# Feed-forward up-projection: high and low part of x in one 512-column matmul

## The chip, the cores and the metric

The kernel runs on one NeuronCore of a Trainium2 chip. The metric is the device time in microseconds (us) from the start to the end of one execution. The core has five engines that work side by side, each through its own queue in order: TensorE (PE; PEld is its loading of weights), VectorE (DVE), ScalarE (ACT), GpSimd (POOL) and SyncE (SP), which issues the DMAs. They meet at semaphores.

## The reference

Two layers of an encoder on 256 tokens of width 1024, in float32. Each layer has a group of attention heads (dense latent attention and dilated windows), with an output projection, and then a gated feed-forward network with a convolution over three neighbouring tokens:

```python
def conv_ffn(h, w_up, conv_w, conv_b, w_down):
    u = h @ w_up                                   # (256, 1024) @ (1024, 2 * 2816)
    u = lax.conv_general_dilated(u, conv_w[:, None, :], window_strides=(1,),
            padding=((1, 1),), feature_group_count=2 * D_FF, ...) + conv_b
    g, up = jnp.split(u, 2, axis=-1)
    return (jax.nn.silu(g) * up) @ w_down          # (256, 2816) @ (2816, 1024)

x = x + conv_ffn(rmsnorm(x, ffn_norm[l]), w_up[l], conv_w[l], conv_b[l], w_down[l])
```

## The kernel before, in words

Every matrix product is made of float32 operands split into a high part, rounded to the matmul's input type, and a low part, the rest. Three matmuls, high x high, high x low and low x high, are added up in one PSUM bank. The weights come from memory in tiles of 1 MB (`raw`); ScalarE makes the high part (`wh`, line 175) and VectorE the low part (`wl`, line 188), unit by unit, with six buffers of each and up to five units ahead of TensorE.

The change lies in the feed-forward stage, which takes some 190 us of each layer. Its 2816 hidden columns are worked in 22 blocks of 128, counted by j. For a block, `up` multiplies the transposed x (`sf.hi`, `sf.lo`, the tiles `xh` and `xl`; 8 k-steps of 128 features by 256 tokens) with the weights of the gate half and of the up half: 2 halves x 8 k-steps x 3 matmuls of 256 columns. Both halves stand side by side in one PSUM bank of 512 columns (only blocks 0 and 1, which begin before all of x is ready, have a bank for each half). Then `gate(j)` evacuates: VectorE multiplies the bank by `r2b`, the scale of the RMS norm for each token, into an SBUF tile of 512 columns; ScalarE applies the middle tap and the bias of the convolution; VectorE adds the other two taps (four operations, line 284), ScalarE applies SiLU, VectorE multiplies gate and up half, and ScalarE and VectorE split the product into high and low part (`mh`, `ml`). `down(j - 3)`, the down-projection of the block three before, follows each `up` on TensorE: 12 matmuls of 512 columns into four accumulators (`acc`). The last four blocks of the down-projection come at the end of the layer.

PSUM has eight banks: four `acc`, two named S (`bank()`), one A (`tbank()`) and one O (`obank()`). Before, the blocks from 3 on alternate between the two S banks, one bank per block. The 512-column SBUF tiles of `wide()` rotate through seven buffers.

Outside the attention part the order of the instructions on each engine is set by a scheduler at build time; it may put weight splits and gate steps in another order when the code changes. Calls of `W.fill` in `gate` offer it the next weight splits.

The helpers `tt` (line 275) and `stt` (284) are VectorE's two-tensor and scalar-two-tensor operations, `act` (287) is ScalarE's, `ptt` (290) POOL's two-tensor operation; a profile shows their lines.

Of the kernel before, what the change touches and what calls it, by code (L numbers as in the profile page):

```python
# [11 lines left out]
F32R = mybir.dt.float32r  # L12
I32 = mybir.dt.int32
AF = mybir.ActivationFunctionType
ALU = mybir.AluOpType
# [4 lines left out]
P = 128  # L20
LINE = 32
D_MODEL = 1024
SEQ = 256
# [9 lines left out]
NF = D_FF // P  # L33
# [198 lines left out]
def encoder(ctx: ExitStack, tc: tile.TileContext, wpk, x, prm, cst, oh, rb, pos, out):  # L232
# [4 lines left out]
    work = ctx.enter_context(tc.tile_pool(name="work", bufs=2))  # L237
# [5 lines left out]
    def nm(s):  # L243
        uid[0] += 1
        return f"{s}_{uid[0]}"

    def wide():
        return work.tile([P, 512], F32, name=nm("t2"), tag="t2", bufs=7)

    def mid():  # L250
        return work.tile([P, 256], F32, name=nm("t1"), tag="t1", bufs=9)
# [4 lines left out]
    def small(n, dt=F32):  # L256
        return work.tile([P, max(n, LINE)], dt, name=nm("s"), tag=f"s{n}_{dt}", bufs=8 if n <= 32 else 2)[:, :n]
# [4 lines left out]
    def bank():  # L262
        return psa.tile([P, 512], F32, name=nm("S"), tag="S", bufs=2)

    def tbank():
        return psa.tile([P, 512], F32, name=nm("A"), tag="A", bufs=1)

    def obank():
        return psa.tile([P, 512], F32, name=nm("O"), tag="O", bufs=1)

    def acc():
        return psa.tile([P, 512], F32, name=nm("acc"), tag="acc", bufs=4)

    def tt(o, a, b, op):
        nc.vector.tensor_tensor(out=o, in0=a, in1=b, op=op)  # L275
# [7 lines left out]
    def stt(o, a, s, b, op0, op1):  # L283
        nc.vector.scalar_tensor_tensor(out=o, in0=a, scalar=s, in1=b, op0=op0, op1=op1)  # L284

    def act(o, a, f, **kw):
        nc.scalar.activation(o, a, f, **kw)  # L287
# [15 lines left out]
    mm = nc.tensor.matmul  # L303
# [145 lines left out]

    def new_xT():  # L450
        s = State()
        s.hi = work.tile([P, 8, SEQ], F32R, name=nm("xh"), tag="xh", bufs=1)
        s.lo = work.tile([P, 8, SEQ], F32R, name=nm("xl"), tag="xl", bufs=1)
        s.ss = small(4)
        return s

# [154 lines left out]
    def layer(l, sx, late, bias):  # L611
# [346 lines left out]
        def d_end(i, t):  # L958
# [8 lines left out]
            2: [lambda: d_end(1, 0), lambda: (d_end(1, 1), d_factor(1, kd))],  # L967
        }
        sf = new_xT()
        gf = par("ffn_norm", l)  # L970
        hd = Heads(l, False, qd, kd, vd, pairs)
# [90 lines left out]
        r2b = work.tile([P, SEQ], F32, name=nm("r2b"), tag="r2b", bufs=1)  # L1062

        def ffn_scale():
            xT_stats(sf)
            ob = obank()
            dg = mid()
            for t in range(2):
                ts(dg[:, t * P:t * P + P], ident, sf.r[:, t:t + 1], ALU.mult)
            mm(ob[:, :SEQ], ones, dg, start=True, stop=True)  # L1070
            act(r2b, ob[:, :SEQ], AF.Copy)
# [4 lines left out]
        def up(j, pu, ks=range(8)):  # L1076
            for half in range(2):
                u = u_f + FFN_AT[("gate", "up")[half], j]
                hi, lo = W.get(u)
                o = pu[half][:, :SEQ] if len(pu) == 2 else pu[0][:, half * SEQ:(half + 1) * SEQ]  # L1080
                for k in ks:
                    kp = slice(k * P, k * P + P)
                    mm(o, hi[:, kp], sf.hi[:, k, :], start=k == 0, stop=False)  # L1083
                    mm(o, hi[:, kp], sf.lo[:, k, :], start=False, stop=False)  # L1084
                    mm(o, lo[:, kp], sf.hi[:, k, :], start=False, stop=k == 7)  # L1085
                if ks[-1] == 7:
                    W.done(u)

        def gate(j, pu):
            s, y = wide(), wide()  # L1090
            if len(pu) == 2:
                for g in range(2):
                    tt(s[:, g * SEQ:(g + 1) * SEQ], pu[g][:, :SEQ], r2b, ALU.mult)
            else:
                tt(s.rearrange("p (g t) -> p g t", g=2), pu[0].rearrange("p (g t) -> p g t", g=2),
                   r2b.unsqueeze(1).to_broadcast([P, 2, SEQ]), ALU.mult)
            for g in range(2):
                b = j + NF * g
                act(y[:, g * SEQ:(g + 1) * SEQ], s[:, g * SEQ:(g + 1) * SEQ], AF.Identity,
                    scale=cw[:, 44 + b:45 + b], bias=cb[:, b:b + 1])  # L1100
            W.fill(2)
            for g in range(2):
                b = j + NF * g
                yg, sg = y[:, g * SEQ:(g + 1) * SEQ], s[:, g * SEQ:(g + 1) * SEQ]
                stt(yg[:, 1:], sg[:, :SEQ - 1], cw[:, b:b + 1], yg[:, 1:], ALU.mult, ALU.add)
                stt(yg[:, :SEQ - 1], sg[:, 1:], cw[:, 88 + b:89 + b], yg[:, :SEQ - 1], ALU.mult, ALU.add)
            sl, gt = mid(), mid()
            act(sl, y[:, :SEQ], AF.Silu)
            W.fill(2)
            tt(gt, sl, y[:, SEQ:], ALU.mult)  # L1110
            m = State()
            m.hi = work.tile([P, 1, SEQ], F32R, name=nm("mh"), tag="mh", bufs=6)
            m.lo = work.tile([P, 1, SEQ], F32R, name=nm("ml"), tag="ml", bufs=6)
            act(m.hi[:, 0, :], gt, AF.Copy)
            W.fill(2)
            tt(m.lo[:, 0, :], gt, m.hi.bitcast(F32)[:, 0, :], ALU.subtract)
            gates[j] = m
# [13 lines left out]
        def down(j):  # L1131
            for t in range(2):
                for c in range(2):
                    down_mm(j, t, c)
            W.done(u_f + FFN_AT["down", j])

        first = [[acc(), acc()], [bank(), bank()]]
        for j in range(2):
            up(j, first[j], range(4))
            W.fill()  # L1140
        xT_part(sf, gf, 0, 1, tbank())
        xT_part(sf, gf, 1, 1, obank())
        for j in range(NF):
            if j < 2:
                pu = first[j]
                up(j, pu, range(4, 8))
            else:
                pu = [tbank() if j == 2 else bank()]
                up(j, pu)
            if j == 0:  # L1150
                ffn_scale()
            gate(j, pu)
            if j == 0:
                box["a"] = [[acc(), acc()], [acc(), acc()]]
            if FFN_LAG <= j < NF + FFN_LAG - FFN_HOLD:
                down(j - FFN_LAG)
        held = list(range(NF - FFN_HOLD, NF))
        last = l == DEPTH - 1
        if not last:
            sx_next = new_xT()  # L1160
            gn = par("attn_norm", l + 1)
# [20 lines left out]
        for j, t, c in order:  # L1182
# [5 lines left out]
            if (j, t, c) in ((held[0], 1, 1), (held[1], 1, 1)):  # L1188
# [3 lines left out]
                         lambda: xT_stats(sx_next)]  # L1192

    s0 = new_xT()
    late = []
    angles = rope_angles()
    bias = [bias_tables]
    for l in range(DEPTH):
        s0, late = layer(l, s0, late, bias)
        bias = []  # L1200
# [57 lines left out]
```

## Time and profile before

| | us |
|---|---|
| median of three runs | 660.03 |
| lowest, highest | 659.01, 660.3 |
| the profiled execution | 659.02 |
| its span in the trace | 657.2 |
| TensorE busy | 636.5 |
| VectorE busy | 493.7 |
| ScalarE busy | 399.6 |
| POOL busy | 67.5 |

The span is the time between the first and the last recorded instruction of the profiled execution. An engine's busy time counts the time in which at least one of its instructions is in progress; a matmul overlaps the next one, so what TensorE needs for one is read from the distance between two starts, not from its duration. Idle time of an engine that nobody waits for costs nothing.

### The profile page before, as it was taken

What the parts mean: (1) busy time and instruction counts of PE and PEld (TensorE: products, weight loads), DVE (VectorE), ACT (ScalarE), POOL (GpSimd) and SP (SyncE); (2) the same over time, 40 slices, a digit from 0 to 9 for tenths busy, and PEclk for the clock granted to TensorE, in tenths of its full rate; (3) what the DMA queues carried; (4) which work ended last, traced back from release to release, by engine and by line L of the source; (5) the groups of instructions that cost most, each with busy time, mean ns of one, the idle gap of its engine ahead of it and who ended that gap; (6) DMA issues with size and microseconds to landing.
All of it is one profiled execution on the core that took longest, in us unless ns stands there. A gap on an engine that the chain in (4) does not pass through costs nothing.

```text
span 657.2 us, 10655 instructions
## 1 busy us (share of the span) xinstructions
PE 636.5 (97%) x4018; PEld 554.3 (84%) x4018; DVE 493.7 (75%) x1006; ACT 399.6 (61%) x721; POOL 67.5 (10%) x177
## 2 busy tenths in 40 slices
PE   8989899989999999999999989999899999999997
PEld 7867676679999999999899876667899999999996
DVE  5796676677987777778699766667699777777773
ACT  6972976756755555555478467766385555555551
POOL 3850170000000000000001105400000000000000
PEclk9999999999999999999999999999899999999999
DMA  8759431252664555554347422313247545544401
GB/s 300 269 194 173 179 128 65 65 192 79 237 207 183 192 193 192 192 177 154 112 136 272 161 78 115 128 65 129 65 168 280 181 175 175 184 189 188 161 1 64
DMA packets 17708, 105.19 MB, mean 160 GB/s; under 512 B 2103, under 2 KB 3800, under 8 KB 6649
## 3 DMA queue, kind: packets, MB, share of 16 engines
q1 hardware_dynamic: 17656, 104.51, 45.9%
q8 instruction: 31, 0.51, 0.3%
q14 instruction: 21, 0.16, 0.1%
HBM read 103.20 MB, written 1.31 MB: 159 GB/s over the span
## 4 chain that ended last, share of the span: by engine, by line
PE 83%; POOL 6%; DVE 5%; ACT 2%; issue 2%; DMA 1%; SPq 1%; DVEq 0%; ACTq 0%; POOLq 0%
PE S L1085 12%; PE S L1084 12%; PE S L1083 12%; PE acc L1129 6%; PE acc L1128 6%; PE acc L1127 6%; PE acc L492 3%; PE acc L491 3%; PE acc L490 3%; PE O L600 3%; POOL s L295 3%; PE S L551 2%; PE A L591 2%; PE acc L935 2%; PE acc L938 2%; PE acc L937 2%
## 5 line engine op out<-in xcount | busy, mean ns | idle before, releaser
L175 ACT ACTIVATE wh<-raw 128x1024 fp32r<-128x1024 f32 (+3 forms) x188 | 193.2, 1036 | 110.6 <-PE S L1084 64.8
L188 DVE TENSOR_TENSOR wl<-raw,wh 128x1024 fp32r<-128x1024 f32 (+3 forms) x188 | 223.6, 1192 | 28.7 <-ACT wh L175 28.1
L1084 PE MATMUL S<-xl,wh 128*128 128x256 f32 x640 | 181.3, 284 | 0.0
L1085 PE MATMUL S<-xh,wl 128*128 128x256 f32 x640 | 180.9, 283 | 0.0
L1083 PE MATMUL S<-xh,wh 128*128 128x256 f32 x640 | 180.3, 283 | 0.0
L1084 PEld LDWEIGHTS S<-xl,wh 128*128 128x128 f32 x640 | 122.7, 192 | 1.5
L1083 PEld LDWEIGHTS S<-xh,wh 128*128 128x128 f32 x640 | 122.4, 192 | 1.6
L1085 PEld LDWEIGHTS S<-xh,wl 128*128 128x128 f32 x640 | 122.7, 192 | 0.1
L284 DVE SCALAR_TENSOR_TENSOR t<-t,prm_s,t 128x255 f32<-128x255 f32 x176 | 74.0, 480 | 1.0 <-ACT t L287 0.9
L1129 PE MATMUL acc<-wl,mh 128*128 128x512 f32 x176 | 69.3, 394 | 0.0
L1127 PE MATMUL acc<-wh,mh 128*128 128x512 f32 x176 | 69.3, 394 | 0.0
L1128 PE MATMUL acc<-wh,ml 128*128 128x512 f32 x176 | 69.2, 393 | 0.0
L490 PE MATMUL acc<-wh,xh 128*128 128x512 f32 (+2 forms) x160 | 61.3, 383 | 0.9 <-ACT nat L287 0.9
L492 PE MATMUL acc<-wl,xh 128*128 128x512 f32 (+2 forms) x160 | 58.2, 364 | 0.4 <-DVE wl L188 0.4
L491 PE MATMUL acc<-wh,xl 128*128 128x512 f32 (+2 forms) x160 | 57.8, 361 | 0.0
L287 ACT ACTIVATE t<-A 128x512 f32<-128x512 f32 (+2 forms) x56 | 28.1, 503 | 45.3 <-PE A L528 23.3
L287 ACT ACTIVATE t<-t,prm_s 128x256 f32<-128x256 f32 x88 | 47.9, 593 | 4.7 <-DVE t L275 4.7
L287 ACT ACTIVATE mh<-t 128x256 fp32r<-128x256 f32 x44 | 18.3, 416 | 47.7 <-DVE t L275 47.7
L275 DVE TENSOR_TENSOR t<-S,r2b 128x512 f32<-128x512 f32 (+1 forms) x42 | 28.0, 666 | 24.0 <-PE S L1085 24.0
L1129 PEld LDWEIGHTS acc<-wl,mh 128*128 128x128 f32 x176 | 33.1, 188 | 7.5
L1127 PEld LDWEIGHTS acc<-wh,mh 128*128 128x128 f32 x176 | 33.4, 190 | 5.9
L1128 PEld LDWEIGHTS acc<-wh,ml 128*128 128x128 f32 x176 | 33.1, 188 | 6.1
(168 smaller groups left out, 974.2 us busy)
## 6 DMA issues: line engine op xcount, KB each, us to landing
raw<-in_wpk_dram SPq DMA_DIRECT2D x86, 1024.0 KB, 4.8
raw<-in_wpk_dram SPq DMA_DIRECT2D x3, 896.0 KB, 4.6
raw<-in_wpk_dram SPq DMA_DIRECT2D x3, 768.0 KB, 4.9
raw<-in_wpk_dram SPq DMA_DIRECT2D x2, 816.0 KB, 5.9
Bn<-scr SPq DMA_DIRECT2D x8, 192.0 KB, 11.3
raw<-in_wpk_dram SPq DMA_DIRECT2D x2, 720.0 KB, 5.6
X<-in_x_dram SPq DMA_DIRECT2D x4, 256.0 KB, 5.3
raw<-in_wpk_dram SPq DMA_DIRECT2D x2, 384.0 KB, 5.6
```

Of the source, the lines that this page charges most:

```text
L175: self.nc.scalar.activation(hi[:, :n], self.raw[t][:, o:o + n], AF.Copy, scale=1.0 if g is None else g)
L188: self.nc.vector.tensor_tensor(out=lo[:, :n], in0=raw, in1=hi, op=ALU.subtract)
L287: nc.scalar.activation(o, a, f, **kw)
L490: mm(o, lhs.hi[:, k, sl], rh, start=k == 0, stop=False)
L491: mm(o, lhs.lo[:, k, sl], rh, start=False, stop=False)
L492: mm(o, lhs.hi[:, k, sl], rl, start=False, stop=k == ktot - 1)
L1083: mm(o, hi[:, kp], sf.hi[:, k, :], start=k == 0, stop=False)
L1084: mm(o, hi[:, kp], sf.lo[:, k, :], start=False, stop=False)
L1085: mm(o, lo[:, kp], sf.hi[:, k, :], start=False, stop=k == 7)
L1127: mm(o, m.hi[:, 0, sl], hi[:, cs], start=j == 0, stop=False)
L1128: mm(o, m.lo[:, 0, sl], hi[:, cs], start=False, stop=False)
L1129: mm(o, m.hi[:, 0, sl], lo[:, cs], start=False, stop=j == NF - 1)
```

## The change

The two parts of x become one tile, `xhl`, so that a k-step's high and low part can be read by one matmul of 512 columns, high part times weight in the left half of the bank and low part in the right half. The product of high x and low weight is added to the left half by a matmul of 256 columns. So a block now takes two banks, one for each half, in which left and right have still to be added: blocks with odd j use the two S banks, those with even j A and O. In `gate`, ScalarE copies the right halves to a new tile `c`, VectorE scales the left halves as before, POOL scales `c` (VectorE for the last two blocks), and the two are added by POOL for even j below 15, by VectorE otherwise.

```diff
@@ -449,8 +449,8 @@
 
     def new_xT():
         s = State()
-        s.hi = work.tile([P, 8, SEQ], F32R, name=nm("xh"), tag="xh", bufs=1)
-        s.lo = work.tile([P, 8, SEQ], F32R, name=nm("xl"), tag="xl", bufs=1)
+        s.both = work.tile([P, 2, 8, SEQ], F32R, name=nm("xhl"), tag="xhl", bufs=1)
+        s.hi, s.lo = s.both[:, 0], s.both[:, 1]
         s.ss = small(4)
         return s
 
@@ -1077,23 +1077,23 @@
             for half in range(2):
                 u = u_f + FFN_AT[("gate", "up")[half], j]
                 hi, lo = W.get(u)
-                o = pu[half][:, :SEQ] if len(pu) == 2 else pu[0][:, half * SEQ:(half + 1) * SEQ]
+                o = pu[half]
                 for k in ks:
                     kp = slice(k * P, k * P + P)
-                    mm(o, hi[:, kp], sf.hi[:, k, :], start=k == 0, stop=False)
-                    mm(o, hi[:, kp], sf.lo[:, k, :], start=False, stop=False)
-                    mm(o, lo[:, kp], sf.hi[:, k, :], start=False, stop=k == 7)
+                    mm(o.rearrange("p (g t) -> p g t", g=2), hi[:, kp], sf.both[:, :, k, :], start=k == 0, stop=False)
+                    mm(o[:, :SEQ], lo[:, kp], sf.hi[:, k, :], start=False, stop=k == 7)
                 if ks[-1] == 7:
                     W.done(u)
 
         def gate(j, pu):
-            s, y = wide(), wide()
-            if len(pu) == 2:
-                for g in range(2):
-                    tt(s[:, g * SEQ:(g + 1) * SEQ], pu[g][:, :SEQ], r2b, ALU.mult)
-            else:
-                tt(s.rearrange("p (g t) -> p g t", g=2), pu[0].rearrange("p (g t) -> p g t", g=2),
-                   r2b.unsqueeze(1).to_broadcast([P, 2, SEQ]), ALU.mult)
+            s, y, c = wide(), wide(), wide()
+            for g in range(2):
+                act(c[:, g * SEQ:(g + 1) * SEQ], pu[g][:, SEQ:], AF.Copy)
+                tt(s[:, g * SEQ:(g + 1) * SEQ], pu[g][:, :SEQ], r2b, ALU.mult)
+            side = tt if j >= NF - 2 else ptt
+            side(c.rearrange("p (g t) -> p g t", g=2), c.rearrange("p (g t) -> p g t", g=2),
+                 r2b.unsqueeze(1).to_broadcast([P, 2, SEQ]), ALU.mult)
+            (tt if j % 2 or j >= NF - 7 else ptt)(s, s, c, ALU.add)
             for g in range(2):
                 b = j + NF * g
                 act(y[:, g * SEQ:(g + 1) * SEQ], s[:, g * SEQ:(g + 1) * SEQ], AF.Identity,
@@ -1145,7 +1145,7 @@
                 pu = first[j]
                 up(j, pu, range(4, 8))
             else:
-                pu = [tbank() if j == 2 else bank()]
+                pu = [bank(), bank()] if j % 2 else [tbank(), obank()]
                 up(j, pu)
             if j == 0:
                 ffn_scale()
```

On TensorE, the end of a down step (acc) and the first k-step of the next block in layer 0 are, before (S is the bank, xh and xl the parts of x, wh and wl those of the weight, mh and ml those of the gate's product):

```order
L1128 MATMUL acc_1941<-wh_2310,ml_2143 128x512
L1129 MATMUL acc_1941<-wl_2325,mh_2142 128x512
L1083 MATMUL S_2438<-xh_894,wh_2323 128x256
L1084 MATMUL S_2438<-xl_895,wh_2323 128x256
L1085 MATMUL S_2438<-xh_894,wl_2400 128x256
L1083 MATMUL S_2438<-xh_894,wh_2323 128x256
```

and now, with the start of the second k-step:

```order
L1128 MATMUL acc_1920<-wh_2250,ml_2101 128x512
L1129 MATMUL acc_1920<-wl_2265,mh_2100 128x512
L1083 MATMUL S_2369<-xhl_893,wh_2263 128x512
L1084 MATMUL S_2369<-xhl_893,wl_2331 128x256
L1083 MATMUL S_2369<-xhl_893,wh_2263 128x512
```

Three matmuls of a k-step have become two, and one of them is of 512 columns.

On VectorE, a block in the middle of layer 0 is, before, from its evacuation (t from S and r2b) to the next one (L188 is a weight split, L284 the convolution's taps, ml the low part of the gate's product):

```order
L275 TENSOR_TENSOR t_491_2579<-S_2530,r2b_1767 128x512
L188 TENSOR_TENSOR wl_2684<-raw_2419,wh_2678 128x1024
L284 SCALAR_TENSOR_TENSOR t_492_2580<-t_491_2579,prm_s,t_492_2580 128x255 x4
L188 TENSOR_TENSOR wl_2697<-raw_2500,wh_2682 128x1024
L275 TENSOR_TENSOR t_494_2599<-t_493_2598,t_492_2580 128x256
L275 TENSOR_TENSOR ml_2609<-t_494_2599,mh_2608 128x256
L188 TENSOR_TENSOR wl_2772<-raw_2500,wh_2695 128x1024
L275 TENSOR_TENSOR t_498_2673<-S_2624,r2b_1767 128x512
```

and now a block with even j (banks A and O; the first row is its second evacuation), with the evacuations of the next, odd one (S) and its add:

```order
L275 TENSOR_TENSOR t_504_2486<-O_2453,r2b_1765 128x256
L188 TENSOR_TENSOR wl_2601<-raw_2422,wh_2586 128x1024
L284 SCALAR_TENSOR_TENSOR t_505_2487<-t_504_2486,prm_s,t_505_2487 128x255 x4
L188 TENSOR_TENSOR wl_2667<-raw_2422,wh_2599 128x1024
L275 TENSOR_TENSOR t_508_2512<-t_507_2511,t_505_2487 128x256
L275 TENSOR_TENSOR t_513_2571<-S_2537,r2b_1765 128x256
L275 TENSOR_TENSOR ml_2522<-t_508_2512,mh_2521 128x256
L275 TENSOR_TENSOR t_513_2571<-S_2538,r2b_1765 128x256
L275 TENSOR_TENSOR t_513_2571<-t_513_2571,t_515_2573 128x512
L188 TENSOR_TENSOR wl_2673<-raw_2501,wh_2665 128x1024
L284 SCALAR_TENSOR_TENSOR t_514_2572<-t_513_2571,prm_s,t_514_2572 128x255 x4
L188 TENSOR_TENSOR wl_2684<-raw_2501,wh_2671 128x1024
```

Evacuations come in twos, the add of the odd block stands between its evacuation and the next weight split, and the low part of the even block stands between the two evacuations of the odd one.

On POOL there was nothing in this stage; the same two blocks and the one behind are now:

```order
L290 TENSOR_TENSOR t_506_2488<-t_506_2488,r2b_1765 128x512
L290 TENSOR_TENSOR t_504_2486<-t_504_2486,t_506_2488 128x512
L290 TENSOR_TENSOR t_515_2573<-t_515_2573,r2b_1765 128x512
L290 TENSOR_TENSOR t_524_2656<-t_524_2656,r2b_1765 128x512
L290 TENSOR_TENSOR t_522_2654<-t_522_2654,t_524_2656 128x512
```

Scale and add of the even block, scale of the odd one (whose add is VectorE's row above), and again.

## Rows read from the trace of the kernel before

**Rows 1.** Page: busy time by engine, and the granted TensorE clock by slice.
```profile
PE 636.5 (97%) x4018; PEld 554.3 (84%) x4018; DVE 493.7 (75%) x1006; ACT 399.6 (61%) x721; POOL 67.5 (10%) x177
PEclk9999999999999999999999999999899999999999
```

**Rows 2.** Stretches: us, their length, then busy time (instructions) of PE, PEld, DVE, ACT, POOL.
```profile
220.00:240.00 20.00, 20.00 (x139) 18.62 (x139) 16.12 (x26) 11.92 (x19) 0.00 (x0) 1.00 0.56 205
480.00:500.00 20.00, 20.00 (x147) 18.96 (x146) 20.00 (x37) 15.60 (x25) 0.00 (x0) 1.00 0.54 190
```

**Rows 3.** Timeline of PE: start, duration, engine, line, operation, count.
```profile
218.89 0.39 PE L1127 MATMUL acc<-wh,mh 128*128 128x512 f32 x1
221.44 0.39 PE L1129 MATMUL acc<-wl,mh 128*128 128x512 f32 x1
221.66 0.28 PE L1083 MATMUL S<-xh,wh 128*128 128x256 f32 x1
227.42 0.39 PE L1127 MATMUL acc<-wh,mh 128*128 128x512 f32 x1
...
636.00 0.39 PE L1129 MATMUL acc<-wl,mh 128*128 128x512 f32 x1
636.22 0.28 PE L1083 MATMUL S<-xh,wh 128*128 128x256 f32 x1
```

**Rows 4.** Groups by line: engine, tiles, shapes, count | busy us, mean ns | idle before.
```profile
L287 ACT ACTIVATE mh<-O 128x256 fp32r<-128x256 f32 x16 | 6.2, 386 | 5.5 <-PE O L600 5.2
L287 ACT ACTIVATE t<-t,prm_s 128x256 f32<-128x256 f32 x88 | 47.9, 593 | 4.7 <-DVE t L275 4.7
L275 DVE TENSOR_TENSOR xl<-t,xh 128x512 fp32r<-128x512 f32 x12 | 8.3, 688 | 0.8 <-ACT xh L287 0.8
L290 POOL TENSOR_TENSOR nat<-nat,fd 128x512 f32<-128x512 f32 x8 | 8.2, 1043 | 0.3
```

**Rows 5.** Timeline of DVE: one block in the middle of the stage.
```profile
253.20 0.69 DVE L275 TENSOR_TENSOR t<-S,r2b 128x512 f32<-128x512 f32 x1 [0.61 <-PE S L1085]
254.17 1.23 DVE L188 TENSOR_TENSOR wl<-raw,wh 128x1024 fp32r<-128x1024 f32 x1 [0.28 <-ACT wh L175]
255.31 1.66 DVE L284 SCALAR_TENSOR_TENSOR t<-t,prm_s,t 128x255 f32<-128x255 f32 x4
256.89 1.22 DVE L188 TENSOR_TENSOR wl<-raw,wh 128x1024 fp32r<-128x1024 f32 x1
258.03 0.42 DVE L275 TENSOR_TENSOR t<-t,t 128x256 f32<-128x256 f32 x1
258.93 0.42 DVE L275 TENSOR_TENSOR ml<-t,mh 128x256 fp32r<-128x256 f32 x1 [0.48 <-ACT mh L287]
259.88 1.23 DVE L188 TENSOR_TENSOR wl<-raw,wh 128x1024 fp32r<-128x1024 f32 x1 [0.53 <-ACT wh L175]
261.72 0.69 DVE L275 TENSOR_TENSOR t<-S,r2b 128x512 f32<-128x512 f32 x1 [0.61 <-PE S L1085]
```

**Rows 6.** Timelines of POOL and DVE where both work.
```profile
91.68 0.24 POOL L290 TENSOR_TENSOR s<-s,s 128x16 f32<-128x16 f32 x1
92.01 1.29 POOL L295 TENSOR_SCALAR s<-s 128x16 f32<-128x16 f32 x1
92.02 1.22 DVE L188 TENSOR_TENSOR wl<-raw,wh 128x1024 fp32r<-128x1024 f32 x1
...
34.56 0.32 POOL L290 TENSOR_TENSOR s<-krs,sing 128x64 f32<-128x64 f32 x1
34.58 0.32 DVE L284 SCALAR_TENSOR_TENSOR s<-s,s 128x2 f32<-128x2 f32 x1
38.34 0.15 DVE L284 SCALAR_TENSOR_TENSOR s<-s,s 128x2 f32<-128x2 f32 x1
```

**Rows 7.** Timeline of DVE: the last gate, from its evacuation to its low part.
```profile
642.18 0.69 DVE L275 TENSOR_TENSOR t<-S,r2b 128x512 f32<-128x512 f32 x1 [2.36 <-PE S L1085]
...
646.48 0.43 DVE L275 TENSOR_TENSOR ml<-t,mh 128x256 fp32r<-128x256 f32 x1 [0.49 <-ACT mh L287]
```

## Prediction

> **What bounds the kernel now.** I read the page's table of busy time first: TensorE is busy for 97% of the span and the granted clock is at its full level in nearly every slice [rows 1]. Then the busy time by stretches, where the share of the feed-forward stage is what matters: in a steady 20 us of it TensorE has no gap at all, VectorE has 16.1, ScalarE 11.9, and GpSimd (POOL) nothing to do; early in that stage VectorE is full as well (20.0 of 20) [rows 2]. So the stage, some 190 us in each layer, runs at TensorE's pace with VectorE as the next in line.
>
> Then the timeline of TensorE. Twelve 512-column matmuls of one down step take 218.89 to 221.66, 2.77 us or 0.231 each; the 48 of 256 columns behind them take until 227.42, 5.76 us or 0.120 each [rows 3]. A feed-forward column block (a j) is 8.53 us. The step from a 512-column matmul to a 256-column one occurs 36 times, from 221.44 to 221.66 first quoted and from 636.00 to 636.22; it is 0.22 or 0.23, 0.227 in the mean [rows 3].
>
> **The change, part by part.** *Matmuls.* Per k-step and half, three matmuls of 0.120 become one of 512 columns and one of 256. A 512 with a 512 behind it takes 0.231, with a 256 behind it 0.227, which is the pairing that the new code has; I take 0.229. A step goes from 0.360 to 0.349, and there are 2 layers x 22 blocks x 2 halves x 8 = 704: 7.7 us saved, with ends of 6.3 (0.231) and 9.2 (0.227). All of it is on the path as long as TensorE stays the bound. A block becomes 16 x 0.349 + 2.77 = 8.35 us.
>
> By the Trainium skill, page "TensorE: Matmul & The Clock Gate", section "Wait — 56ns, not 53.3ns?", a warm matmul costs its columns over 2.4 GHz plus about 2.5 ns: that is 109 ns and 216 ns, and a merge of two would save only the 2.5 ns, an estimated 1.8 us in all. The rows have 120 and 231, so its numbers don't fit this data type; by its rule the change would be lost in the noise.
>
> *Banks.* The two halves of a block now take two banks, and two pairs (S, S and A, O) alternate, so a pair has to be empty when the block after next begins: two down steps and one up, 2.77 + 5.58 + 2.77 = 11.1 us after its matmuls. Before, one S bank alternated with the other, with the same distance.
>
> *ScalarE* gets two 256-column copies out of a bank per block; the nearest row is 386 ns [rows 4]: 0.8 us, on 5.1 of 8.5 (11.9 of 20) [rows 2]. It stays under TensorE.
>
> *VectorE.* The 0.69 evacuation becomes two of 256 columns (a 256-column operation is 0.42, and 0.34 from issue to issue, since neighbours overlap by 0.09: 254.17 + 1.23 against 255.31) [rows 5]. Blocks with odd j, and all from 15 on, get an add of 512 columns in SBUF, 0.69 [rows 4], 0.60 issue to issue; blocks 20 and 21 the multiplication too.
>
> *POOL* gets a 512-column multiplication for blocks 0 to 19 and an add for the even ones up to 14; the row is 1.04 us [rows 4]. Alone that is 3.1 us per pair of blocks. But a 16-column POOL operation that takes 0.24 takes 1.29 when a weight split starts with it on VectorE, and is over 0.06 after the split [rows 6]: it waits until the split is done. The other direction is shown only small: a 2-column VectorE operation takes 0.32 beside a POOL operation of 0.32, against 0.15 elsewhere [rows 6]. If that holds for a long one, VectorE and POOL take turns.
>
> That is what the Trainium skill says, page "SBUF — State Buffer", section "Who interferes with whom": a VectorE operation with two SBUF inputs and a POOL operation that reads SBUF exclude each other for a whole instruction. The trace agrees for POOL's wait (1.29 against 0.24).
>
> So I walk a pair of blocks (even, then odd) through the order of the queues. VectorE's own issue distances: 6 weight splits x 1.14, 8 scalar-tensor operations in 2 x 1.58 (255.31 to 256.89), 2 products, 2 low parts and 4 evacuations x 0.34, one add 0.60: 13.3 us. Three POOL operations, 3.1. Together 16.4 against TensorE's pair of 16.7. On top come waits in queue order: the even block's convolution cannot start until copy, POOL product, POOL add and a ScalarE step (0.4 + 1.04 + 1.04 + 0.6) [rows 4] are through, with only two splits to fill that time. Behind the waiting convolution stand the next splits and the next block's evacuation; behind ScalarE's step, which waits for the add, stand the next high part (five units ahead, so TensorE does not feel it) and the SiLU. In the walk the pair comes to 16.3 us where a POOL operation that waits gets the next turn, and to 17.1 where VectorE's next split slips in ahead of it. I take the first. From block 15 on the POOL add is gone and a pair is 15.9.
>
> *Start of the stage.* VectorE is already full there [rows 2]. From the end of block 0's gate half TensorE needs 15.6 us to the end of block 3 (1.4 + 2.8 + 0.2 + 2 x 5.6). VectorE, from one high part (1.1) later, has in the new order 8 splits (9.1), 3 convolutions (4.7), 13 operations of 0.34 (4.4) and an add (0.6) to issue before that block's evacuation is done, 18.8, and five POOL operations (5.2) take turns with it, about four fifths of them outside its other waits: 24 us, or 8.5 behind the matmuls, inside the 11.1. Block 3 itself waits about 0.5 us for block 1's banks; against it, TensorE no longer waits for the second half of x, transposed earlier now. I cost the start at 0 (-0.6 to +1.3 a layer).
>
> *End of the layer.* The last gate took 642.18 to 646.91 before, 4.7 us [rows 7]; with a multiplication and an add on VectorE it is 6.1 behind the last matmul. TensorE has nine groups of three down matmuls (0.69 each) to fill 6.2 us, so the chain as such is just hidden, but every us that VectorE is still behind counts. It is 8.5 behind at block 3, gains 0.4 per pair up to block 14 (2.2), 0.8 per pair from 15 to 19 (2.0), and about 2 in the last two, which have short splits and no POOL: 2.2 us are left and show as a wait of TensorE at the end of each layer. With pairs of 17.1 it loses 1.9 instead of gaining 2.2, and 6.4 are left. Without the taking of turns nothing is left.
>
> **Sum.** 7.7 saved, 2 x 2.2 given back: -3.3. The profiled execution took 659.02 us (span 657.2); it becomes 655.7. The median of the runs is 660.03, 1.0 above the profiled one, so the forecast is 656.7. Its own range is 654 to 658.7 (savings of 6.3 to 9.2, a wait of 1.5 to 3 a layer).
>
> **Rivals.** *Slower: POOL and VectorE take turns the bad way.* Pairs at 17.1 leave 6.4 us at the end of each layer, and blocks early in the stage wait for banks too (1.3 a layer): -7.7 + 2 x (6.4 + 1.3) = +7.7, or 668; without the bank waits 665. It decides from a pair of 16.7, TensorE's own. For it: 16.4 us of work against 16.7 leaves no room for a wait, and long chains now pass through three in-order queues. Against it: odd blocks need POOL for one operation only, and from 15 on there is room.
>
> *Full gain.* VectorE does not really wait for POOL (only 0.17 us of such a wait is in the trace), or POOL's operations fall into VectorE's waits: VectorE then has 13.3 plus some 2 us of waits in 16.7, catches up as it does now, and the saving stands: -6.3 to -9.2, or 652.
>
> *Nothing.* The merged matmul reads two pieces 2048 columns apart and is written over two halves; if that costs 5 ns more, or if the pair is 16.6 and the end of the layers takes 3.5 each, the time stays at 660. For it: every extra microsecond at a layer's end is paid whole. The skill's rule on matmul cost would end here too.
>
> **How the numbers follow.** Forecast 0.42, full gain 0.20, nothing 0.16, slower 0.22. About 0.2%, 1.3 us, is what a measurement of this kernel can tell from no change: below 658.7 is faster (forecast and full gain), 658.7 to 661.3 the same, above slower: 0.62, 0.16, 0.22. The range reaches from the full gain's middle, 651, to 664.5, which holds the milder half of the slower case.
>
> **What would show it.** Right: in the new profile the distance from the 512-column to the 256-column matmul of an up step is 0.227 to 0.231 and back 0.120; up steps take about 5.6 us; POOL's 512-column operations show durations well over 1.04; VectorE's evacuations trail the matmuls by some 8 us in the middle of the stage; TensorE has its one wait in the stage at the end of each layer, for the last gate's parts, about 2 us. Wrong: gaps of TensorE in the middle of the stage, waiting for banks or low weight parts (slower); evacuations right behind the matmuls and no wait at the end (full gain); a distance of 0.24 behind the 512-column matmul (nothing).

## The result: slower, because GpSimd's second operation waits for another turn

The changed kernel takes 667.0 us (median of 4 runs, 666.06 to 668.87), the kernel before, run beside it, 659.56: a ratio of 1.0118, 95% interval 1.0102 to 1.0134. The forecast was 656.7, with a range from 651 to 664.5. The profiled execution took 666.99 us, its span is 665.2 (before 657.2, so +8.0).

The page of the changed kernel, busy time and the granted clock of TensorE by slice, against [rows 1]:

```profile
PE 635.4 (96%) x3314; PEld 517.9 (78%) x3314; DVE 529.9 (80%) x1078; ACT 422.9 (64%) x809; POOL 168.4 (25%) x233
PEclk9999999999999999999899989999999999999998
```

Stretches, with columns as in [rows 2]:

```profile
220.00:240.00 20.00, 20.00 (x106) 17.01 (x104) 15.85 (x24) 10.73 (x19) 8.07 (x5) 1.00 0.58 201
480.00:500.00 20.00, 19.09 (x106) 16.27 (x105) 18.17 (x27) 12.83 (x23) 9.27 (x5) 1.00 0.56 206
```

In a steady 20 us TensorE still has no gap, and the clock is full; the 0.91 missing from 480 to 500 are block 3's wait for block 1's banks, forecast at 0.5. VectorE is busy for *less* of that stretch than before (15.85 against 16.12) although it has more to do: it waits, while POOL is busy for 8.07.

TensorE's timeline, against [rows 3]: one block into the banks A and O, from its first matmul to the down step behind it, then one into S:

```profile
221.84 0.40 PE L1083 MATMUL A<-xhl,wh 128*128 128x512 f32 x1
222.07 0.28 PE L1084 MATMUL A<-xhl,wl 128*128 128x256 f32 x1
222.19 0.39 PE L1083 MATMUL A<-xhl,wh 128*128 128x512 f32 x1
...
227.39 0.39 PE L1127 MATMUL acc<-wh,mh 128*128 128x512 f32 x1
...
230.17 0.39 PE L1083 MATMUL S<-xhl,wh 128*128 128x512 f32 x1
...
235.81 0.39 PE L1127 MATMUL acc<-wh,mh 128*128 128x512 f32 x1
```

The distances are the forecast's: 0.23 behind the 512-column matmul, 0.12 behind the other. An up step takes 5.55 us (227.39 - 221.84) or 5.64 (235.81 - 230.17), a pair of blocks 16.77, where it took 17.05. So the matmuls gave what they should, and the loss is elsewhere. TensorE's timeline from 318 to 339 us, behind layer 0's last up step, has these waits in its down matmuls, and between them slower matmuls:

```profile
325.84 0.50 PE L1127 MATMUL acc<-wh,mh 128*128 128x512 f32 x1 [3.25 <-ACT mh L287]
...
328.29 0.63 PE L1127 MATMUL acc<-wh,mh 128*128 128x512 f32 x1
328.71 0.63 PE L1128 MATMUL acc<-wh,ml 128*128 128x512 f32 x1
...
332.13 0.74 PE L1127 MATMUL acc<-wh,mh 128*128 128x512 f32 x2 [0.77 <-ACT mh L287]
```

The kernel before has no such wait there. TensorE waits for the high parts of late gates' products, first block 20's, then block 21's, the last. Behind the first wait its matmuls come up to 0.43 apart instead of 0.23, until 330.28: from 327 to 330 the granted clock is 0.50, its lower level (1.2 GHz), after 3.25 us without a matmul. This makes some 1.9 us, but costs next to nothing of its own here, since TensorE still has to wait for the last gate behind it (0.77 in layer 0, 0.21 in layer 1). The bill of the two spans, from the starts in TensorE's timeline (us):

| | layer 0 | layer 1 |
|---|---|---|
| last down run of the layer (start to end), before | 12.18 | 11.31 |
| the same, changed | 18.51 | 17.39 |
| given back at the end | +6.3 | +6.1 |
| first down step to last down run, before | 153.48 | 153.48 |
| the same, changed | 150.90 | 150.90 |
| saved in the middle | -2.6 | -2.6 |
| all before the first down step | +1.0 | -0.3 |

Together +8.0, the whole difference of the spans. The last row holds the attention part too.

Why the gates are late is read from one pair of blocks. VectorE's timeline shows the second evacuation of two odd blocks, two blocks apart:

```profile
227.36 0.42 DVE L275 TENSOR_TENSOR t<-S,r2b 128x256 f32<-128x256 f32 x1
...
244.61 0.42 DVE L275 TENSOR_TENSOR t<-S,r2b 128x256 f32<-128x256 f32 x1
```

The gates' loop takes 17.25 us for a pair (17.24 in the mean of four pairs), TensorE 16.77: each pair the gates fall 0.47 behind. Between those rows lies an even block. VectorE, POOL and ScalarE, in order of time:

```profile
235.27 1.22 DVE L188 TENSOR_TENSOR wl<-raw,wh 128x1024 fp32r<-128x1024 f32 x1
235.57 2.07 POOL L290 TENSOR_TENSOR t<-t,r2b 128x512 f32<-128x512 f32 x1 [6.93 <-ACT t L287]
236.41 0.42 DVE L275 TENSOR_TENSOR t<-O,r2b 128x256 f32<-128x256 f32 x1
236.74 1.98 DVE L188 TENSOR_TENSOR wl<-raw,wh 128x1024 fp32r<-128x1024 f32 x1
237.72 2.15 POOL L290 TENSOR_TENSOR t<-t,t 128x512 f32<-128x512 f32 x1
239.91 1.09 ACT L287 ACTIVATE t<-t,prm_s 128x256 f32<-128x256 f32 x2 [3.46 <-POOL t L290]
240.54 0.48 DVE L284 SCALAR_TENSOR_TENSOR t<-t,prm_s,t 128x255 f32<-128x255 f32 x1 [1.82 <-ACT t L287]
```

Read it by ends. POOL's scaling begins while a split runs, gets on when that is done (236.49) and ends at 237.64. The next split, begun at 236.74, waits for the scaling and then runs from 237.64 to 238.72: 1.98 instead of 1.22. POOL's add begins at 237.72, 0.08 after the scaling; by then the split has the turn, so the add waits until 238.72 and ends at 239.87. ScalarE has waited 3.46, and VectorE, whose queue has nothing but the convolution next, stands idle for 1.82. The groups hold all such operations (1.04 alone, [rows 4]). The scalings take 1.29 in most odd blocks and 2.07 in most even ones, the adds 2.15, but 3.61 for the first of each layer:

```profile
L290 POOL TENSOR_TENSOR t<-t,r2b 128x512 f32<-128x512 f32 x40 | 64.0, 1599 | 225.8 <-ACT t L287 214.2 <-issue 11.5
L290 POOL TENSOR_TENSOR t<-t,t 128x512 f32<-128x512 f32 x16 | 37.3, 2333 | 6.9 <-DVE t L275 6.0
```

### The profile page after: what moved, and what is told of

Its sections match the earlier page's. It is cut to its first block, busy times and chain, and to the rows that moved or that the text cites. A ratio compares the mean times of both kernels' runs of the same rounds, so it can differ in the third digit from the quotient of the medians.

```text
span 665.2 us, 9525 instructions
## 1 busy us (share of the span) xinstructions
PE 635.4 (96%) x3314; PEld 517.9 (78%) x3314; DVE 529.9 (80%) x1078; ACT 422.9 (64%) x809; POOL 168.4 (25%) x233
## 5 line engine op out<-in xcount | busy, mean ns | idle before, releaser
L188 DVE TENSOR_TENSOR wl<-raw,wh 128x1024 fp32r<-128x1024 f32 (+3 forms) x188 | 233.0, 1243 | 6.8 <-ACT wh L175 6.8
L1083 PE MATMUL S<-xhl,wh 128*128 128x512 f32 x352 | 124.9, 397 | 1.8 <-DVE t L275 1.8
L290 POOL TENSOR_TENSOR t<-t,r2b 128x512 f32<-128x512 f32 x40 | 64.0, 1599 | 225.8 <-ACT t L287 214.2
L284 DVE SCALAR_TENSOR_TENSOR t<-t,prm_s,t 128x255 f32<-128x255 f32 x176 | 81.0, 514 | 23.5 <-ACT t L287 23.3
L1084 PE MATMUL S<-xhl,wl 128*128 128x256 f32 x352 | 98.7, 280 | 0.0
L1083 PEld LDWEIGHTS S<-xhl,wh 128*128 128x128 f32 x352 | 66.0, 188 | 17.9 <-PE O L1084 2.4
L1084 PEld LDWEIGHTS S<-xhl,wl 128*128 128x128 f32 x352 | 66.5, 189 | 0.9
L490 PE MATMUL acc<-wh,xhl 128*128 128x512 f32 (+2 forms) x160 | 61.6, 385 | 0.9 <-ACT nat L287 0.9
L492 PE MATMUL acc<-wl,xhl 128*128 128x512 f32 (+2 forms) x160 | 58.2, 364 | 1.0 <-DVE wl L188 1.0
L491 PE MATMUL acc<-wh,xhl 128*128 128x512 f32 (+2 forms) x160 | 58.0, 362 | 0.1
L1083 PE MATMUL O<-xhl,wh 128*128 128x512 f32 x160 | 57.0, 395 | 0.0
L1083 PE MATMUL A<-xhl,wh 128*128 128x512 f32 x160 | 56.8, 395 | 0.0
L1084 PE MATMUL O<-xhl,wl 128*128 128x256 f32 x160 | 44.9, 280 | 0.0
```

The costliest lines, as they stand in the source:

```text
L188: self.nc.vector.tensor_tensor(out=lo[:, :n], in0=raw, in1=hi, op=ALU.subtract)
L290: nc.gpsimd.tensor_tensor(out=o, in0=a, in1=b, op=op)
L490: mm(o, lhs.hi[:, k, sl], rh, start=k == 0, stop=False)
L492: mm(o, lhs.hi[:, k, sl], rl, start=False, stop=k == ktot - 1)
L1083: mm(o.rearrange("p (g t) -> p g t", g=2), hi[:, kp], sf.both[:, :, k, :], start=k == 0, stop=False)
L1084: mm(o[:, :SEQ], lo[:, kp], sf.hi[:, k, :], start=False, stop=k == 7)
```

## The experiments

Theory 1: VectorE and POOL take turns, the second POOL operation of an even block always loses one to a split, so the gates' loop is slower than TensorE and the lag is paid at each layer's end. Rivals: the gate's chain or VectorE's load is simply too large (2); the loss is in the start, the copies or the banks (3); only the last gate's chain is not covered (4); the two engines' work adds up, and the order doesn't matter (5). Medians are of 4 runs (10 where said), ratios are to the kernel before run beside them; the two kernels of their own, on turns, ran once each.

**No POOL.** Both side operations on VectorE:

```diff
-            side = tt if j >= NF - 2 else ptt
+            side = tt
-            (tt if j % 2 or j >= NF - 7 else ptt)(s, s, c, ALU.add)
+            tt(s, s, c, ALU.add)
```

> The changed kernel with both side operations of a gate (the scaling of the right halves, the add) on VectorE in every block; POOL has nothing in the stage. Theory 1 (VectorE and POOL shut each other out, a pair of blocks takes 17.24 us against TensorE's 16.77, the lag is paid as a wait at each layer's end): VectorE's pair is 13.3 + 3 x 0.6 = 15.1, below 16.77, although VectorE does more; the lag and most of the 6.3 and 6.1 us at the two ends go: 655 to 658. Theory 2 (the gate has simply become too long a chain, or VectorE too full, POOL or not): VectorE has 1.8 us more in a pair, so 665 to 670.

653.51 us, ratio 0.9909 (0.9886 to 0.9933), 1.5 below theory 1's range. VectorE does more and the kernel is some 13 us faster than the changed one: theory 2 falls. I had expected a remainder of the wait at the ends; layer 1's last down run is back at 11.35. TensorE's waits, longest first in total (engine, its line, what it waited for; us, times, longest), have `mh` no more:

```profile
PE A L528 <- DVE t L279: 4.9, 6, 1.0
PE A L431 <- DVE X L275: 3.8, 2, 1.9
```

In the changed kernel that view begins

```profile
PE acc L1127 <- ACT mh L287: 7.6, 4, 3.3
```

**No side operations.**

```diff
-            side = tt if j >= NF - 2 else ptt
-            side(c.rearrange(...), c.rearrange(...), r2b..., ALU.mult)
-            (tt if j % 2 or j >= NF - 7 else ptt)(s, s, c, ALU.add)
```

> The changed kernel without the scaling of the right halves and without the add (these are left out of the computation: high weight times low x is lost); ScalarE still copies the right halves out, the banks are arranged as in the changed kernel. Theory 1: no POOL, VectorE's pair is 12.7, nothing is left at the layers' ends: 653 to 655, which is all that the merged matmuls can give. Theory 3 (the time is lost at the stage's start, in ScalarE's copies or in the arrangement of the banks): 660 or more.

652.42 us, 0.9891 (0.9864 to 0.9919), 0.6 below theory 1's range: 6.8 us below before with copies and banks as in the changed kernel. This kernel leaves out the scaling and the add. Theory 3 falls; this is about all that the matmuls can give.

**More down blocks held.**

```diff
-FFN_HOLD = 4
+FFN_HOLD = 5
```

> The changed kernel with five blocks of the down-projection held for the end of the layer instead of four. Theory 1 (the gates' loop is late because VectorE with POOL is slower than TensorE over the whole stage): VectorE's end decides, and moving TensorE's work moves it by one weight split at most, 1.1 us a layer: 664.5 to 667. Theory 4 (the loop is in time and only the last gate's chain, 6.1 us, is not covered by TensorE's nine groups of matmuls): three groups of 0.69 more cover 2.1 us a layer: 662.5 to 663.5.

667.98 us, 1.0131 (1.0105 to 1.0157), 1 above theory 1's range and 4.5 above theory 4's. Three more groups of matmuls ahead of the last gate gave nothing; TensorE only reaches its wait earlier, and the wait is longer:

```profile
325.46 0.79 PE L1127 MATMUL acc<-wh,mh 128*128 128x512 f32 x1 [4.57 <-ACT mh L287]
```

It ends at 325.46 where it ended at 325.84: the gates' loop sets that moment. It is a wait for the last block but one, so more than the last gate is late, and by that theory 4 falls. The time alone does not show it: the wait for the last gate is in fact gone (two waits for `mh` in the whole run instead of four), and what eats that gain is the clock behind the longer wait (granted 0.50 from 325 to 330): ten 512-column matmuls in 4.78 us (325.46 to 330.24), where they take 2.3 at the full clock.

**The add off POOL.**

```diff
-            (tt if j % 2 or j >= NF - 7 else ptt)(s, s, c, ALU.add)
+            tt(s, s, c, ALU.add)
```

> The changed kernel with the add on VectorE in every block; POOL only scales the right halves. Theory 1: eight POOL operations of each layer go, those that wait behind a weight split for 2.2 us and keep ScalarE's step and the convolution waiting; VectorE 13.9 + POOL 2.1 = 16.0 for a pair, some waits on top: about TensorE's pace, 658 to 662. Theory 2 (VectorE too full): 0.6 more in a pair, 668 to 670.

654.73 us, 0.9929 (0.9903 to 0.9955), better than theory 1's 658 to 662. Eight adds a layer make some 12 us. The even block now, VectorE and POOL, and the odd blocks' evacuations:

```profile
222.34 0.42 DVE L275 TENSOR_TENSOR t<-S,r2b 128x256 f32<-128x256 f32 x1
...
230.31 1.22 DVE L188 TENSOR_TENSOR wl<-raw,wh 128x1024 fp32r<-128x1024 f32 x1
230.66 2.00 POOL L290 TENSOR_TENSOR t<-t,r2b 128x512 f32<-128x512 f32 x1 [6.99 <-ACT t L287]
231.44 0.42 DVE L275 TENSOR_TENSOR t<-O,r2b 128x256 f32<-128x256 f32 x1
232.69 0.69 DVE L275 TENSOR_TENSOR t<-t,t 128x512 f32<-128x512 f32 x1 [0.84 <-POOL t L290]
...
238.40 0.42 DVE L275 TENSOR_TENSOR t<-S,r2b 128x256 f32<-128x256 f32 x1
```

POOL's scaling waits for a split as before (2.00), but the add no longer does; the pair is 16.06 (238.40 - 222.34), below 16.77, and the gates catch up.

**The add on POOL in odd blocks too.**

```diff
-            (tt if j % 2 or j >= NF - 7 else ptt)(s, s, c, ALU.add)
+            (tt if j >= NF - 2 else ptt)(s, s, c, ALU.add)
```

> The changed kernel with the add on POOL in every block but the last two, the odd ones too. In the changed kernel a pair of blocks (one add on POOL) takes 17.24 us, with no add on POOL 16.06. Theory 1, turns: an add that comes to POOL right behind the scaling it depends on finds a VectorE split waiting, which gets the turn first, so each such add adds about 1.2 us to the pair: 18.4 us, 1.2 more than the changed kernel in seven pairs and 2.3 more in the two and a half behind them, 14 us a layer, part of it in TensorE waiting for banks: 690 to 696. Theory 5, sums: the work of the two engines adds up and nothing else: VectorE 12.7 + POOL 4.2 = 16.9 for a pair, no slower than the changed kernel: 662 to 667.

694.15 us, 1.0519 (1.0498 to 1.0539). Theory 1's numbers; theory 5 is 27 us off. In the middle of the stage TensorE waits not for banks, as I had expected, but for the low weight parts of a late VectorE (9.0 us in 12 waits). The evacuations of two even blocks, 18.46 apart (theory 1: 18.4):

```profile
239.48 0.42 DVE L275 TENSOR_TENSOR t<-O,r2b 128x256 f32<-128x256 f32 x1
...
257.94 0.42 DVE L275 TENSOR_TENSOR t<-O,r2b 128x256 f32<-128x256 f32 x1
```

**The add alone on POOL.**

```diff
-            side = tt if j >= NF - 2 else ptt
+            side = tt
```

> The changed kernel with the scaling of the right halves on VectorE in every block; POOL has the add of the even blocks below 15 and nothing else. Theory 1: only one POOL operation stands in the chain of an even block, and none in an odd one; VectorE 14.5 + POOL 1.04, and one wait of POOL for a split: 15.6 to 16.7 for a pair, at or below TensorE's 16.77: 653 to 657. If an add on POOL costs its 1.2 us and more whatever stands ahead of it (the add as such), the pair is 15.1 (all on VectorE) + 1.2 + 1.0 of VectorE's waits = 17.3 and the time 664 or more.

658.32 us (10 runs), 0.9982 (0.9969 to 0.9995): 1.3 above theory 1's range, 5.7 below the rival's. The pair is 16.97, a little over TensorE's, and layer 1's last down run 13.08. A single POOL add in the chain still waits for one split and leaves VectorE idle:

```profile
235.01 1.22 DVE L188 TENSOR_TENSOR wl<-raw,wh 128x1024 fp32r<-128x1024 f32 x1
235.26 2.12 POOL L290 TENSOR_TENSOR t<-t,t 128x512 f32<-128x512 f32 x1 [13.70 <-DVE t L275]
237.41 1.09 ACT L287 ACTIVATE t<-t,prm_s 128x256 f32<-128x256 f32 x2 [2.50 <-POOL t L290]
238.05 0.48 DVE L284 SCALAR_TENSOR_TENSOR t<-t,prm_s,t 128x255 f32<-128x255 f32 x1 [1.82 <-ACT t L287]
```

So it matters where a POOL operation stands. Directly ahead of ScalarE's step and the convolution it leaves VectorE idle for 1.82; with VectorE's add behind it, as in the kernel with the add off POOL, for 0.84.

**POOL beside the kernel before.**

```diff
+            d = wide()
+            ptt(d..., s..., r2b..., ALU.mult)
+            if j % 2 == 0:
+                ptt(d, s, d, ALU.add)
```

> The kernel before, with POOL operations added whose result nobody uses: one multiplication of 512 columns in each block and an add in the even ones, on the evacuated tile. The same number of POOL operations as in the changed kernel, but nothing waits for them. Theory 1 in its narrow form (the work of VectorE and of POOL adds up): 12.6 + 3.1 = 15.7 against TensorE's 17.05 for a pair, so no more than 1 us is lost: 659 to 661; it takes the chain through POOL as well to lose the pace. If exclusion alone slows VectorE beyond that (each POOL operation costs VectorE more than its own 1.04): 663 or more. Theory 2: 659 to 660, with VectorE's operations no longer than before.

682.92 us, 1.0363 (1.0342 to 1.0384). The narrow form is wrong by far: operations that nobody waits for cost 24 us. The pair of blocks is 18.01 (247.14 - 229.13):

```profile
229.13 0.68 DVE L275 TENSOR_TENSOR t<-S,r2b 128x512 f32<-128x512 f32 x1
...
238.22 1.21 DVE L188 TENSOR_TENSOR wl<-raw,wh 128x1024 fp32r<-128x1024 f32 x1
238.45 2.14 POOL L290 TENSOR_TENSOR t<-t,r2b 128x512 f32<-128x512 f32 x1 [6.34 <-DVE t L275]
239.35 3.74 DVE L284 SCALAR_TENSOR_TENSOR t<-t,prm_s,t 128x255 f32<-128x255 f32 x4
240.67 1.35 POOL L290 TENSOR_TENSOR t<-t,t 128x512 f32<-128x512 f32 x1
...
247.14 0.68 DVE L275 TENSOR_TENSOR t<-S,r2b 128x512 f32<-128x512 f32 x1
```

Four taps take 3.74 here instead of 1.66 [rows 5]: 2.08 more, twice POOL's 1.04. My 12.6 + 3.1 left out VectorE's waits for ScalarE, 0.48 and 0.53 a block as in [rows 5], and the overlap of 0.08 with the next operation that is lost at each of them: 2.3 for a pair, and with it the sum is 18.0. This kernel also takes one more of the seven rotating SBUF tiles per gate; VectorE has no wait for one in this pair.

**Turns by themselves.** The first kernel wrote all splits to one tile (the stretch "split"; the others differ in VectorE's instruction):

```python
for i in range(24):
    nc.vector.tensor_tensor(out=dv, in0=X, in1=g, op=ALU.subtract)
for i in range(6):
    nc.gpsimd.tensor_tensor(out=po, in0=X[:, :512], in1=g[:, :512], op=ALU.mult)
```

> A kernel of its own, without the reference's computation: four stretches. In each VectorE gets 24 independent instructions back to back; in the last three POOL gets 6 independent multiplications of 512 columns at the same moment. VectorE's instructions: weight splits of 1024 columns alone (solo), the same beside POOL (split), evacuations of 512 columns with one input from PSUM (evac), the convolution's taps of 256 columns (taps). If a POOL operation that waits gets the next turn (as the prediction chose), VectorE's and POOL's instructions alternate, one of POOL to one of VectorE, and POOL's six are done after about 6 x (1.14 + 1.04) = 13 us. If VectorE's next instruction slips in ahead, POOL's six come through late, the last near or behind the end of VectorE's 24 (27 us), each but the first of them lasting far over 1.04. Without exclusion POOL's six are done after 6.3 us. In the stretch evac the same, if an evacuation with one SBUF input also excludes.

The second wrote them to three in turn:

```diff
+        for i in range(8):
+            for d in (d1, d2, d3):
+                nc.vector.tensor_tensor(out=d, in0=X, in1=g, op=ALU.subtract)
+        nc.gpsimd.tensor_tensor(out=po, in0=X[:, :512], in1=g[:, :512], op=ALU.mult)
+        for i in range(5):
+            nc.gpsimd.tensor_tensor(out=po, in0=po, in1=g[:, :512], op=ALU.add)
```

> A kernel of its own, without the reference's computation: 24 splits of 1024 columns back to back on VectorE, written to three tiles in turn so that neighbours can overlap; alone (solo), beside 6 independent POOL multiplications of 512 columns (free), beside a chain of 6 POOL operations each of which reads the result of the one before (chain). In the earlier kernel of this kind, where all splits wrote one tile, POOL and VectorE took strict turns (2.20 us for a split and a multiplication). Theory 1 expects strict turns here too, in the chain as well: 13 us for the six, VectorE's row 6 x 1.04 = 6.2 us longer than alone. If a back-to-back VectorE keeps the turn, POOL's six end at about 27 us.

Strict turns in both, which is the case that the prediction chose. The groups of the first one (24 VectorE instructions in each stretch):

```profile
L251 DVE TENSOR_TENSOR dv_split<-X,g_solo 128x1024 f32<-128x1024 f32 x24 | 35.1, 1461 | 2.4 <-ACT g_solo L262 1.6
L251 DVE TENSOR_TENSOR dv_solo<-X,Y 128x1024 f32<-128x1024 f32 x24 | 29.4, 1225 | 6.2 <-DMA Y<-in_x_dram 5.5
L253 DVE TENSOR_TENSOR dv_evac<-S,g_split 128x512 f32<-128x512 f32 x24 | 16.6, 691 | 3.1 <-ACT g_split L264 2.3
L259 POOL TENSOR_TENSOR po_evac<-X,g_split 128x512 f32<-128x512 f32 x6 | 7.6, 1266 | 25.2 <-ACT g_split L264 24.8
```

The timeline of the second, where a chain of POOL operations begins beside back-to-back splits:

```profile
69.87 1.23 DVE L248 TENSOR_TENSOR d_chain<-X,g_free 128x1024 f32<-128x1024 f32 x1 [1.90 <-ACT g_free L260]
69.92 2.30 POOL L253 TENSOR_TENSOR po_chain<-X,g_free 128x512 f32<-128x512 f32 x1 [22.33 <-ACT g_free L260]
71.01 2.28 DVE L248 TENSOR_TENSOR d_chain<-X,g_free 128x1024 f32<-128x1024 f32 x1
72.30 2.12 POOL L255 TENSOR_TENSOR po_chain<-po_chain,g_free 128x512 f32<-128x512 f32 x1
73.22 2.28 DVE L248 TENSOR_TENSOR d_chain<-X,g_free 128x1024 f32<-128x1024 f32 x1
```

A split gets its turn at the end of each POOL operation, before POOL's next one, whether that is free or chained: 2.20 us for one of each, and POOL's six end after 13.3 us. VectorE's 24 take 33.73 us with POOL and 27.34 alone: 6.4 more, or 1.07 for each POOL operation. Evacuations from PSUM are not held up (0.69 each, as in [rows 5]), while POOL takes 1.27 for each of its own beside them.

**The add ahead of the scaling.** VectorE adds bank and copy, then one scaling, on VectorE or on POOL (the diff), or on VectorE for each half right behind its add:

```diff
-                tt(s[:, g * SEQ:(g + 1) * SEQ], pu[g][:, :SEQ], r2b, ALU.mult)
+                tt(s[:, g * SEQ:(g + 1) * SEQ], pu[g][:, :SEQ], c[:, g * SEQ:(g + 1) * SEQ], ALU.add)
-            side(c.rearrange(...), c.rearrange(...), r2b..., ALU.mult)
-            (tt if j % 2 or j >= NF - 7 else ptt)(s, s, c, ALU.add)
+            side(s.rearrange(...), s.rearrange(...), r2b..., ALU.mult)
```

On VectorE:

> The changed kernel with the add done first, by VectorE, between the left half in the bank and ScalarE's copy of the right half (two operations of 256 columns in place of the two evacuations), and then one scaling of 512 columns in SBUF, on VectorE. Theory 1: VectorE's pair is 13.3 - 0.6 + 1.2 = 13.9, no POOL: 654 to 656. Theory 2 (the chain of the gate has one ScalarE step ahead of the evacuation): 661 or more.

On POOL:

> The changed kernel with the add done first, by VectorE, from the bank and ScalarE's copy, and then one scaling of 512 columns, on POOL (VectorE in the last two blocks): one POOL operation in a block, which stands in the gate's chain. Theory 1: VectorE 12.7 + POOL 2.1 = 14.8 for a pair; if POOL waits behind a split in each block the chain is 1.2 longer but the loop has room: 655 to 659. If every POOL operation of the chain costs a turn as the adds of the changed kernel do: 661 to 665.

On VectorE by halves:

> The add done first by VectorE from the bank and ScalarE's copy, and the scaling behind it, both for each half on its own (256 columns), no POOL: the gate half is through before the up half's matmuls end, so the last gate's chain is shorter. If the end of the layer still has a wait without POOL, 1 us less than the version with one scaling of 512 columns: 651 to 652.5. If TensorE is the bound to the end, the same 652 to 653.5.

652.68 us (0.9898, 0.9872 to 0.9924), 653.71 (0.9908, 0.9878 to 0.9938) and 652.44 (0.9892, 0.9873 to 0.991): all beat both kernels, and each other by nothing that can be told. The first two are 1.3 below theory 1's ranges, the third lies in both of its own. One POOL operation in every block is affordable: the pair is 16.3 there. The halves gave nothing, as when TensorE is the bound to the end: layer 1's last down run is 11.31 with one scaling and 11.33 by halves, 11.31 before.

The readings side by side (pair of blocks: evacuation to evacuation, layer 0; VectorE's own work in a pair as the expectations sum it; last down run: layer 1, before 11.31):

| | POOL operations per pair | VectorE's own work, us | pair, us | last down run, us | median, us |
|---|---|---|---|---|---|
| changed kernel | 3 | 13.3 | 17.24 | 17.39 | 667.0 |
| add on POOL in odd blocks too | 4 | 12.7 | 18.46 | 21.06 | 694.15 |
| add alone on POOL | 1 | 14.5 | 16.97 | 13.08 | 658.32 |
| scaling alone on POOL | 2 | 13.9 | 16.06 | 11.42 | 654.73 |
| add first, scaling on POOL | 2 | 12.7 | 16.3 | 11.64 | 653.71 |

TensorE's pair is 16.77: above it the time is lost, below it not. The number of POOL operations does not order the rows. What a pair has beyond VectorE's own work is 1.1 for each scaling with VectorE's add behind it, 1.8 (add first) and 2.5 (add alone) for one directly ahead of ScalarE's step, and 2.9 for two in a row ((18.46 - 12.7) / 2). The changed kernel has one of the first kind and one of the last, and 13.3 + 1.1 + 2.9 is its 17.3. The place alone does not decide either: the add-first kernel has its POOL operation in the bad place in every block and keeps TensorE's pace, because VectorE has 1.8 us less to do there than with the add alone on POOL.

## Why the prediction was wrong, step by step

- *Matmuls*: the distances came as read. The size was somewhat high: 2.58 us in the 18 blocks of the middle is 6.3 for all 44 blocks, against 7.7 (range 6.3 to 9.2). The kernels without POOL in the gate gain 5.7 to 6.8.
- *ScalarE, the banks*: right. ScalarE stays under TensorE.
- *Start*: +1.0 and -0.3 (with the attention part), inside -0.6 to +1.3.
- *The walk*: this step failed. It offered 16.3 "where a POOL operation that waits gets the next turn" and 17.1 "where VectorE's next split slips in ahead of it", and I took the first. Those are not two rules. Turns are strict, and just for that reason the split comes in: when the scaling ends it is the split that waits, and the add is issued 0.08 later. The pair took 17.24. The rule of the Trainium skill that I weighed (page "SBUF — State Buffer", section "Who interferes with whom": the engine that begins first keeps the shared reading path for a whole instruction) agrees, split 1.98 against 1.22 and POOL's add 2.15 against 1.04; I did not apply it to VectorE's queue between two dependent POOL operations. No run keeps both POOL operations of an even block and takes the split from between them, so the price of that turn by itself is read from the rows (the add waits 1.00) and not measured. The 0.24 that I set against 1.29 for POOL's wait is the row of another operation; the waiting one, a TENSOR_SCALAR of 16 columns, takes 0.21 elsewhere, so the reading stands.
- *End of the layer*: the term was 2.2 a layer for pairs of 16.3 and 6.4 for pairs of 17.1. It is 6.3 and 6.1. The way there was the slower rival's too: a block's second evacuation ended 9.7 us behind its last matmul at block 3 of layer 0, 7.6 at block 5, 10.7 at block 16 and 7.3 at block 21, where I had 8.5, 1.9 more by block 14, and 6.4 left. So the mechanism, place and price of the slower rival (665 to 668) were right, and its chance of 0.22 too small; that 16.4 us of work in 16.7 leave no room for a wait was on the page as the argument for it, and outweighed what I set against it.

## What to carry to other kernels

Where VectorE had long SBUF operations queued back to back, each GpSimd operation with two SBUF inputs cost VectorE its own duration (1.07) and waited up to one VectorE instruction itself; two dependent GpSimd operations in a row waited twice. Count turns along the chain in queue order, not busy shares: with the side operations on the idle engine the kernel was some 13 us slower than with all of them on the busy one. And look at what TensorE does behind a wait: behind the 3.25 us here its matmuls took nearly twice as long (0.43 against 0.23). Adding the bank's halves before scaling removes one operation altogether.

## What the hardware showed that I had not expected

POOL work that nobody waits for is not free: 33 operations in a layer cost the kernel before 12 us a layer. An evacuation that reads PSUM is not held up by POOL (0.69 in the stretch of its own, 0.42 within POOL's scaling above), unlike splits and taps. The same section of the Trainium skill (page "SBUF — State Buffer", section "Who interferes with whom") states that a VectorE instruction with at most one SBUF input, outside the modes that use two ports, does not contend with GpSimd; for VectorE these rows agree, but POOL took 1.27 beside it against 1.04 in [rows 4], so here the measurement decides. In the changed kernel an up step takes 5.64 us in odd blocks (banks S) and 5.55 in even ones (A and O), with the same matmuls; with no POOL operation in the gates it is the other way round, 5.55 into S and 5.64 into A and O, so the bank is not the cause, and no run here says what is.
